# Gate and up projections as seven half-size products per unit in place of eight, and the down projection in four parts

## The chip, the cores and the metric

The kernel runs on one core of a Trainium2 chip. The metric is the device time of one execution in microseconds. The engines are named as in the profile: PE is the matrix engine (PEld its weight loads), DVE the vector engine, ACT the scalar engine, POOL the general-purpose engine, SP the engine that issues most transfers.

## The reference

One inference step of a decoder trunk with two layers, 1024 channels and 576 tokens (512 of a prompt, 64 of samples), all in float32:

```python
for l in range(2):
    x = x + 0.5 * swiglu(rms_norm(x, ffn1_norm[l]), ffn1_w_gu[l], ffn1_w_down[l])
    # l = 0: dilated attention and causal pooling between one input and one output projection
    # l = 1: gated width-3 convolution between two projections
    x = x + mixer(rms_norm(x, mix_norm[l]))
    x = x + 0.5 * swiglu(rms_norm(x, ffn2_norm[l]), ffn2_w_gu[l], ffn2_w_down[l])
y = rms_norm(x, final_norm)

def swiglu(x, w_gu, w_down):             # w_gu 1024 x 5632, w_down 2816 x 1024
    g, u = jnp.split(x @ w_gu, 2, axis=-1)
    return (jax.nn.silu(g) * u) @ w_down
```

So there are four SwiGLU halves, called F1 to F4 here, in the order F1, mixer (attention and pooling), F2, F3, convolution, F4, final norm.

## The kernel before

Activations lie feature-major: `x` is [128 channels, 8 channel tiles, 576 tokens]. Every product runs in reduced-precision float32 passes on exact splits: a weight tile w is split into wh (a cast on ACT, L61) and wl = w − wh (a subtraction on DVE, L62), the activations likewise into `xh` (ACT, L161) and `xl` (DVE, L162), and each product is the three passes wh·xh + wh·xl + wl·xh. A matmul has a 128 x 128 weight and 288 tokens (`C`), so a full product of 1024 input channels and 128 output channels is 8 channel tiles x 3 passes x 2 token halves = 48 matmuls (`proj` and `part`, L220).

A SwiGLU half (`ffn`) has 22 hidden tiles j of 128 channels. For each j there is one 48-matmul product for gate and one for up. `evac` multiplies both by the token factor r of the RMS norm, applies SiLU and multiplies them (L264 to L267), and splits the result into `hh` (ACT) and `hl` (POOL, L269). After 11 hidden tiles come 8 output tiles d of the down projection, 66 matmuls each (11 hidden tiles x 3 x 2), whose result is added to x with the factor one half (L294). So a SwiGLU half is 2 x (11 x 96 + 8 x 66) = 3168 matmuls. In the second half of it, each d also gives its squares to POOL and its split for the next phase to ACT and DVE (`split_x`).

The norm's factor is not needed for the product itself, since it multiplies the result. `norm` sums the squares over channels with four matmuls on PE (L183) and takes the root on ACT and DVE. It is called behind the first product of a phase, and its result is first used in `evac`. In F1 the program start does this by token tiles instead (`tok_factor`, `first_factors`), and the first two products run channel tile by channel tile while x comes in (`first_pair`, L239).

The order of the work on each engine is the order in which the code is written; each engine takes its instructions in that order and waits where a tile is not ready. Weights come by `Weights.load` on SP into two buffers of 1 MB, and are split two tiles ahead of their use. PSUM holds four accumulators of two banks. The last two output tiles of F4 are done by token halves (`last_down`, L330), so that the final norm of the first half lies beside the products of the second.

Of the kernel before, what the change touches and what calls it, by code (L numbers as in the profile page):

```python
# [26 lines left out]
NEG = -1e36  # L27
TOKS = [slice(128 * j, min(128 * j + 128, NT)) for j in range(5)]
# [4 lines left out]
class Weights:  # L33
    """The stream of weight tiles in order of use: loads run ahead, splits two chunks ahead."""

    def __init__(self, nc, raw_pool, split_pool, units):
        self.nc, self.raw_pool, self.split_pool = nc, raw_pool, split_pool
        self.units = units
        self.chunks = []
        for u, (ap, cols, parts) in enumerate(units):  # L40
            o = 0
            for n in parts:
                self.chunks.append((u, o, n, o + n == cols))
                o += n
        self.raw = {}
        self.ready = {}
        self.last = None
        self.n_load = self.n_split = self.n_used = 0
# [7 lines left out]

    def tiles(self):
        return [self.split_pool.tile([128, 1024], F32R, tag=n, name=n) for n in ("wh", "wl")]

    def parts(self, src, h, l, v):  # L60
        self.nc.scalar.copy(out=h[:, v], in_=src)  # L61
        self.nc.vector.tensor_tensor(out=l[:, v], in0=src, in1=h[:, v].bitcast(F32), op=ALU.subtract)  # L62

    def first(self):
        """the first unit, a quarter of both its chunks at a time: (load, split)"""
        ap = self.units[0][0].rearrange("p (c n) -> p c n", c=2)
        t = self.raw_pool.tile([128, 2048], F32, tag="raw", name="raw").rearrange("p (c n) -> p c n", c=2)
        self.ready = {c: self.tiles() for c in range(2)}
        self.n_load, self.n_split = 1, 2

        def load(i):
            v = slice(256 * i, 256 * i + 256)
            self.nc.sync.dma_start(out=t[:, :, v], in_=ap[:, :, v])

        def split(i):
            v = slice(256 * i, 256 * i + 256)
            for c in range(2):
                self.parts(t[:, c, v], *self.ready[c], v)

        return load, split  # L80

    def split(self):
        u, o, n, last = self.chunks[self.n_split]
        if u not in self.raw:
            self.load()
        final = self.last is not None and self.n_split == len(self.chunks) - 1
        h, l = self.ready[self.n_split] = self.last if final else self.tiles()
        self.parts(self.raw[u][:, o:o + n], h, l, slice(0, n))
        self.n_split += 1
        if last:  # L90
            del self.raw[u]
            self.load()

    def next(self, ahead=2):
        while self.n_split <= min(self.n_used + ahead, len(self.chunks) - 1):
            self.split()
# [3 lines left out]


def ch(t):
    """[p, 576] as [p, 2, 288]"""
# [3 lines left out]
class Trunk:  # L107
    def __init__(self, ctx, tc, I, O, phases):
# [5 lines left out]
        self.ps = ctx.enter_context(tc.tile_pool(name="ps", bufs=4, space=PSUM))  # L114
# [6 lines left out]
        self.gain = cp.tile([128, 7, KD], F32, name="gain")  # L121
        self.ones = cp.tile([128, 128], F32, name="ones")
# [5 lines left out]
        g = lambda ap: ap.rearrange("p a b -> p (a b)")  # L128
# [1015 lines left out]
```

## Time and profile before

| | before |
|---|---|
| median of three runs | 2355.4 us |
| the three runs | 2355.1, 2355.4, 2358.45 us |
| profiled execution, span of its instructions | 2358.6 us |
| profiled execution, outside the span | the page shows nothing there; the slowest of the runs is about as long as the span |
| PE busy | 98% of the span |
| DVE, ACT, POOL busy | 45%, 27%, 21% |
| mean granted clock of PE | 0.993 |
| moved by transfers | 217.89 MB |

Busy shares are averages over the whole span. PE works nearly without a break, so what sets the time is the number of matmuls and how closely they follow each other, and every pause of PE adds to the end. The mean duration of one matmul in the profile (some 0.3 us) overlaps its neighbours; the step from one start to the next is what a matmul costs.

### The profile page before, as it was taken

The page shows a single profiled execution, that of the slowest core. Times are in us where ns is not written, and L with a number is a line of the kernel's source. Part 1 is how long each engine was busy: PE and PEld are TensorE (multiplying, and loading weights), DVE is VectorE, ACT ScalarE, POOL GpSimd, SP SyncE. Part 2 cuts the span into 40 slices and gives each one's busy share as a digit, 9 for nine tenths or more (in the row PEclk, how much of TensorE's full clock was granted, in tenths as well). Part 3 has the DMA queues.
Part 4 walks back from the last instruction along what each step waited for, and adds up shares of the span by engine and source line. Part 5 has one row for each costly group of instructions (what it writes and reads, how often), then busy time and mean ns, then how long its engine had stood idle before and what let it go on. Part 6 is the DMA issues. An engine that isn't in the chain of part 4 may idle for free.

```text
span 2358.6 us, 39984 instructions
## 1 busy us (share of the span) xinstructions
PE 2323.2 (98%) x17517; PEld 2292.0 (97%) x17517; DVE 1067.6 (45%) x1462; ACT 635.3 (27%) x965; POOL 498.1 (21%) x490
## 2 busy tenths in 40 slices
PE   8999999999999999999999999999999999999998
PEld 8999999999888899999999999999999999999998
DVE  5432344526666754333435533333554563323334
ACT  4221222223334332212222322222221232212222
POOL 2100012308555641100113010011322231000112
PEclk9999999999999999999999999999999999999999
DMA  4222212443334422223222222221222222222222
GB/s 149 75 75 93 90 67 76 154 157 106 127 126 138 130 72 90 79 74 108 72 69 103 85 71 74 102 78 67 98 91 72 91 79 83 73 82 93 85 69 70
DMA packets 70910, 217.89 MB, mean 92 GB/s; under 512 B 14224, under 2 KB 37776, under 8 KB 54096
## 3 DMA queue, kind: packets, MB, share of 16 engines
q1 hardware_dynamic: 70304, 215.24, 27.5%
q8 instruction: 137, 2.24, 0.4%
q14 instruction: 37, 0.30, 0.0%
q10 hardware_dynamic: 432, 0.10, 0.0%
HBM read 204.22 MB, written 11.10 MB: 91 GB/s over the span
## 4 chain that ended last, share of the span: by engine, by line
PE 93%; DVE 5%; issue 1%; POOL 1%; DMA 0%; ACT 0%; SPq 0%; POOLq 0%; DVEq 0%; ACTq 0%
PE acc L220 86%; PE acc L651 3%; PE acc L749 1%; DVE wl L62 1%; DVE U L776 1%; DVE P L804 1%; PE acc L763 1%; PE acc L655 0%; PE acc L849 0%; PE acc L239 0%; DVE xl L162 0%; PE acc L330 0%; PE acc L826 0%; DVE me L789 0%; DMA raw<-in_gu 0%
## 5 line engine op out<-in xcount | busy, mean ns | idle before, releaser
L220 PE MATMUL acc<-xh,wh 128*128 128x288 f32 x3744 | 804.4, 296 | 0.0
L220 PE MATMUL acc<-xl,wh 128*128 128x288 f32 x3744 | 801.9, 295 | 0.4 <-POOL xl L996 0.4
L220 PE MATMUL acc<-xh,wl 128*128 128x288 f32 x3744 | 801.9, 295 | 0.0
L62 DVE TENSOR_TENSOR wl<-raw,wh 128x1024 fp32r<-128x1024 f32 (+3 forms) x389 | 517.0, 1331 | 573.1 <-ACT wh L61 572.0
L220 PEld LDWEIGHTS acc<-xh,wh 128*128 128x128 f32 x3744 | 603.8, 188 | 4.3 <-ACT P L741 1.8
L220 PEld LDWEIGHTS acc<-xl,wh 128*128 128x128 f32 x3744 | 604.1, 188 | 0.7 <-POOL xl L996 0.6
L220 PEld LDWEIGHTS acc<-xh,wl 128*128 128x128 f32 x3744 | 604.2, 188 | 0.0
L61 ACT CAST wh<-raw 128x1024 fp32r<-128x1024 f32 (+3 forms) x389 | 367.0, 945 | 680.8 <-PE acc L220 613.4
L269 POOL TENSOR_TENSOR hl<-t,hh 128x576 fp32r<-128x576 f32 x88 | 126.1, 1433 | 1287.6 <-ACT hh L268 1258.5
L220 PE MATMUL acc<-hl,wh 128*128 128x288 f32 x1364 | 292.1, 296 | 0.0
L220 PE MATMUL acc<-hh,wl 128*128 128x288 f32 x1364 | 292.1, 296 | 0.0
L220 PE MATMUL acc<-hh,wh 128*128 128x288 f32 x1364 | 292.0, 296 | 0.0
L220 PEld LDWEIGHTS acc<-hh,wl 128*128 128x128 f32 x1364 | 219.8, 189 | 0.0
L220 PEld LDWEIGHTS acc<-hh,wh 128*128 128x128 f32 x1364 | 219.8, 189 | 0.0
L220 PEld LDWEIGHTS acc<-hl,wh 128*128 128x128 f32 x1364 | 219.7, 189 | 0.0
L266 DVE TENSOR_TENSOR t<-acc,r 128x576 f32<-128x576 f32 x88 | 66.7, 758 | 312.6 <-PE acc L220 312.6
L268 ACT CAST hh<-t 128x576 fp32r<-128x576 f32 x88 | 59.3, 674 | 397.0 <-DVE t L267 397.0
L294 DVE SCALAR_TENSOR_TENSOR x<-acc,x 128x576 f32<-128x576 f32 x62 | 47.0, 758 | 159.1 <-PE acc L220 159.1
L265 ACT ACTIVATE t<-t 128x576 f32<-128x576 f32 x88 | 60.3, 686 | 179.2 <-DVE t L264 179.2
L156 POOL TENSOR_TENSOR sqt<-x 128x576 f32<-128x576 f32 x33 | 37.9, 1149 | 184.1 <-DVE x L294 158.8
L161 ACT ACTIVATE xh<-x,gain 128x576 fp32r<-128x576 f32 x48 | 36.9, 776 | 141.5 <-DVE x L294 101.4
L267 DVE TENSOR_TENSOR t<-t,t 128x576 f32<-128x576 f32 x88 | 66.8, 759 | 9.2
(220 smaller groups left out, 1581.4 us busy)
## 6 DMA issues: line engine op xcount, KB each, us to landing
raw<-in_gu SPq DMA_DIRECT2D x87, 1024.0 KB, 4.9
raw<-in_dn SPq DMA_DIRECT2D x64, 704.0 KB, 4.1
raw<-in_wqk SPq DMA_DIRECT2D x12, 1024.0 KB, 4.9
raw<-in_cv SPq DMA_DIRECT2D x12, 1024.0 KB, 4.9
kv<-in_kb SPq DMA_DIRECT2D x32, 256.0 KB, 4.3
kv<-in_vb SPq DMA_DIRECT2D x32, 256.0 KB, 4.7
raw<-in_wv SPq DMA_DIRECT2D x6, 1024.0 KB, 5.2
raw<-in_wo SPq DMA_DIRECT2D x4, 1024.0 KB, 4.8
```

What stands on the lines that cost most here:

```text
L61: self.nc.scalar.copy(out=h[:, v], in_=src)
L62: self.nc.vector.tensor_tensor(out=l[:, v], in0=src, in1=h[:, v].bitcast(F32), op=ALU.subtract)
L156: nc.gpsimd.tensor_tensor(out=t, in0=self.x[:, k, :], in1=self.x[:, k, :], op=ALU.mult)
L161: nc.scalar.activation(out=self.xh[:, k, :], in_=self.x[:, k, :], func=AF.Copy, scale=gcol)
L220: nc.tensor.matmul(out=p[:, c, :C], lhsT=w, rhs=m[:, k0 + k, c * C:c * C + C], start=(first and k == 0 and z == 0), stop=(last and k == kn ...
L265: nc.scalar.activation(out=t1, in_=t1, func=AF.Silu)
L266: nc.vector.tensor_tensor(out=t2, in0=pu[:, :, :C], in1=r, op=ALU.mult)
L267: nc.vector.tensor_tensor(out=t2, in0=t2, in1=t1, op=ALU.mult)
L268: nc.scalar.copy(out=ch(hh[:, j, :]), in_=t2)
L269: nc.gpsimd.tensor_tensor(out=ch(hl[:, j, :]), in0=t2, in1=ch(hh[:, j, :].bitcast(F32)), op=ALU.subtract)
L294: nc.vector.scalar_tensor_tensor(out=xd, in0=p[:, :, :C], scalar=0.5, in1=xd, op0=ALU.mult, op1=ALU.add)
L651: nc.tensor.matmul(out=outs[i], lhsT=self.tok(x[:, kk, :], toks[i]), rhs=w, start=(kk == 0 and z == 0), stop=(kk == 7 and z == 2))
```

## The change

The 1024 x 256 block of weights of a hidden tile (gate and up side by side) and the 1024 x 576 activations are each cut into 2 x 2 blocks: 512 input channels by 128 output channels, and 512 input channels by 288 tokens. The product of two such blocked matrices is formed with seven block products in place of eight. The activation side needs seven "forms", sums and differences of the blocks of x (B11, B21, B22 and T1 to T4), each split into a high and a low part. They are made once for a SwiGLU half. The weight side needs sums of the four weight blocks (`sums`), made for every hidden tile on DVE, and their splits: a (two plain blocks), e and f (two sums each), and d (`dsplit`, one plain block).

A hidden tile is now a `unit` of seven block products of 12 matmuls each (`seven`, L352): 84 matmuls in place of 96. In a steady unit their order is B11, T4 of the unit before, B21, T1, T2, B22, T3. Bank 0 of the accumulator x takes B11 and then B21 on top (`a`), bank 1 takes T1 and then B22 (`f`), and a separate bank B takes a copy of B11's result made by ACT (L392), and then T2, T3 and T4 on top. So gate of the first token half is `a`, and the three others are sums of what the banks hold at different times; ACT copies `f` and B aside in between (L416, L418). `gate0` (L399) reads `a` on DVE. In the first unit of each part there is no unit before, and the order is B11, T1, B21, T2, B22, T3, with `gate0` behind T2 in the code.

The down projection is done in four parts (CHUNKS, of 5, 5, 6 and 6 units), each with 8 output tiles d of 30 or 36 matmuls. The first two d leave out the last unit's hidden tile until T4 of it is done. The result of a d is multiplied by `rm` (a row of −r/2, since h carries the other sign) and added to x by two DVE instructions (L504, L505) in place of one. The norm's factor comes by token tiles in every SwiGLU half (`factor_sums`, `newton`, `factor`), inside its first unit. Squares are on ACT, their sums on POOL. PSUM is three accumulators of two banks and two single banks.

```diff
+CHUNKS = ((0, 5), (5, 5), (10, 6), (16, 6))
...
+    def sums(self, u):
...
+        tt(out=b[:, 0:2], in0=r[:, 0:4:2], in1=r[:, 2:4], op=ALU.add)
+        tt(out=b[:, 2], in0=b[:, 1], in1=r[:, 0], op=ALU.add)
+        tt(out=b[:, 3], in0=b[:, 2], in1=r[:, 1], op=ALU.add)
...
+    def dsplit(self, u):
+        h, l = (self.dpool.tile([128, 512], F32R, tag=n, name=n) for n in ("dh", "dl"))
+        self.parts(self.raw[u][:, 1536:2048], h, l)
...
+    def hi_lo(self, hl, src, g):
...
+        nc.scalar.activation(out=hl[0], in_=src, func=AF.Copy, scale=g)
+        nc.vector.scalar_tensor_tensor(out=hl[1], in0=src, scalar=g, in1=hl[0].bitcast(F32), op0=ALU.mult, op1=ALU.subtract)
+    def forms_low(self, k, n, xb, tmp, eng=None):
...
+        self.hi_lo(self.form("B11", k), x0, g)
+        nc.scalar.activation(out=xb, in_=x1, func=AF.Copy, scale=g)
+        (eng or nc.vector).tensor_tensor(out=tmp, in0=x0, in1=x1, op=ALU.subtract)
+        self.hi_lo(self.form("T1", k), tmp, g)
+    def forms_high(self, k, n, xb, st):
...
+        self.hi_lo(self.form("B21", k), x0, g)
+        stt(out=st[:, 0], in0=x1, scalar=g, in1=xb, op0=ALU.mult, op1=ALU.subtract)
+        stt(out=st[:, 1], in0=self.x[:, k, :C], scalar=ngk, in1=st[:, 0], op0=ALU.mult, op1=ALU.subtract)
+        stt(out=st[:, 2], in0=x0, scalar=ng, in1=st[:, 1], op0=ALU.mult, op1=ALU.subtract)
+    def forms_main(self, k, n, st):
...
+        nc.scalar.copy(out=h, in_=st)
+        nc.vector.tensor_tensor(out=l, in0=st, in1=h.bitcast(F32), op=ALU.subtract)
+        self.hi_lo(self.form("B22", k), self.x[:, k + 4, C:], self.gain[:, n, k + 4:k + 5])
...
+    def seven(self, out, name, w, col, first, last):
...
+        for k in range(4):
+            v = slice(col + 128 * k, col + 128 * k + 128)
+            fh, fl = self.form(name, k)
+            for z, (a, m) in enumerate(((h, fh), (h, fl), (l, fh))):
+                nc.tensor.matmul(out=out, lhsT=a[:, v], rhs=m, start=(first and k == 0 and z == 0),
+                                 stop=(last and k == 3 and z == 2), skip_group_check=True)
+    def half_mult(self, s):
...
+        tt(out=s["h"][:, C:], in0=s["B"][:, :C], in1=s["p5"], op=ALU.add)
+        tt(out=s["h"][:, C:], in0=s["h"][:, C:], in1=s["g"][:, C:], op=ALU.mult)
+    def finish_unit(self, s):
...
+        self.seven(s["B"][:, :C], "T4", s["d"], 0, False, True)
+        nc.vector.tensor_tensor(out=s["h"][:, :C], in0=s["B"][:, :C], in1=s["g"][:, :C], op=ALU.mult)
+    def unit(self, u, j, prev, fresh, start):
...
+        x = self.acc()
+        a, f, b = x[:, 0, :C], x[:, 1, :C], self.psb.tile([128, 512], F32, tag="B", name="B")
...
+        if prev:
+            self.half_mult(prev)
+        wa = W.take()
+        self.seven(a, "B11", wa, 0, True, False)
+        W.ahead(1)
+        nc.scalar.copy(out=b[:, :C], in_=a)
+        if prev:
+            self.finish_unit(prev)
+            s["d"] = W.dsplit(u)
+            self.hidden_parts(prev)
+        def gate0():
+            tt(out=g0, in0=a, in1=r[:, :C], op=ALU.mult)
+            nc.scalar.activation(out=g0, in_=g0, func=AF.Silu)
+        if prev:
+            self.seven(a, "B21", wa, 512, False, True)
+            gate0()
+        we = W.take()
+        self.seven(f, "T1", we, 0, True, False)
+        if start:
+            self.factor_sums()
+        if not prev:
+            s["d"] = W.dsplit(u)
+            self.seven(a, "B21", wa, 512, False, True)
+        W.sums(u + 1)
+        W.ahead(1)
+        if start:
+            self.newton(*self.fa)
+        nc.scalar.copy(out=s["p5"], in_=f)
+        self.seven(b[:, :C], "T2", we, 512, False, False)
+        nc.scalar.copy(out=u2, in_=b[:, :C])
+        if start:
+            self.factor()
+        if not prev:
+            gate0()
+        wf = W.take()
+        self.seven(f, "B22", wf, 512, False, True)
+        tt(out=g1, in0=f, in1=u2, op=ALU.add)
+        tt(out=g1, in0=g1, in1=r[:, C:], op=ALU.mult)
+        W.ahead(1)
+        nc.scalar.activation(out=g1, in_=g1, func=AF.Silu)
+        self.seven(b[:, :C], "T3", wf, 0, False, False)
...
+    def factor(self):
...
+        self.spread(outs, f, TOKS)
+        nc.scalar.copy(out=self.r[:, 0:512], in_=p[:, 0, :])
+        nc.scalar.copy(out=self.r[:, 512:], in_=p[:, 1, :64])
+        nc.vector.tensor_scalar(out=self.rm, in0=self.r, scalar1=-0.5, scalar2=None, op0=ALU.mult)
...
+    def ffn(self, i, u0):
...
+            self.half_mult(s)
+            held = []
...
+            for d in range(8):
...
+                if d < 2:
+                    self.down_part(p, w, 0, kc - 1, kc)
+                    held.append((d, p, w))
+                    if d == 0:
+                        self.finish_unit(s)
+                        self.hidden_parts(s)
+                        s = None
+                        continue
+                    for d, p, w in held:
+                        self.down_part(p, w, kc - 1, 1, kc)
+                else:
+                    self.down_part(p, w, 0, kc, kc)
+                    held = [(d, p, w)]
+                for d, p, w in held:
+                    self.down_out(d, p, last, nxt, kind)
...
+    def down_out(self, d, p, last, nxt, kind):
...
+        nc.vector.tensor_tensor(out=ch(t), in0=p[:, :, :C], in1=ch(self.rm), op=ALU.mult)
+        nc.vector.tensor_tensor(out=xd, in0=xd, in1=t, op=ALU.add)
```

How the instructions stand on an engine is decided by this code's order. Three places on DVE follow. First, a steady unit (the second and third of F1). Before, for each hidden tile, with two weight tiles' subtractions (L62), the two evacuations and their product:

```order
L62 TENSOR_TENSOR wl<-raw,wh 128x1024 x2
L264 TENSOR_TENSOR t_544<-acc,r 128x576
L266 TENSOR_TENSOR t_545<-acc,r 128x576
L267 TENSOR_TENSOR t_545<-t_545,t_544 128x576
L62 TENSOR_TENSOR wl<-raw,wh 128x1024 x2
```

After, from the subtraction of f of one unit (sum, `wl`) over the evacuation of T4 (L365), the subtraction of d, `gate0` (L399), the sums for the next unit (L103 to L105), the subtraction of the next a, the evacuation of B22 (L425, L426), the subtraction of the next e, and the addition that opens the next unit (L358):

```order
L93 TENSOR_TENSOR wl<-sum,wh 128x1024
L365 TENSOR_TENSOR h<-B,g 128x288
L93 TENSOR_TENSOR dl<-raw,dh 128x512
L399 TENSOR_TENSOR g<-acc,r 128x288
L103 TENSOR_TENSOR sum<-raw 128x1024
L104 TENSOR_TENSOR sum<-sum,raw 128x512
L105 TENSOR_TENSOR sum<-sum,raw 128x512
L93 TENSOR_TENSOR wl<-raw,wh 128x1024
L425 TENSOR_TENSOR g<-acc,u_384 128x288
L426 TENSOR_TENSOR g<-g,r 128x288
L93 TENSOR_TENSOR wl<-sum,wh 128x1024
L358 TENSOR_TENSOR h<-B,p_383 128x288
```

Five instructions per hidden tile have become thirteen (L359, a product behind L358, is not among these rows), and `gate0`, for which PE's T1 waits (it writes the other bank of the same accumulator), stands behind T4's evacuation and d's subtraction.

Second, the end of F2, where x is prepared for F3. Before, for one output tile d: its evacuation (L294), its split (L162), and the subtractions of the weights that come next:

```order
L62 TENSOR_TENSOR wl<-raw,wh 128x768
L62 TENSOR_TENSOR wl<-raw,wh 128x640
L294 SCALAR_TENSOR_TENSOR x<-acc,x 128x576
L162 SCALAR_TENSOR_TENSOR xl<-x,gain,xh 128x576
L62 TENSOR_TENSOR wl<-raw,wh 128x1024 x2
L294 SCALAR_TENSOR_TENSOR x<-acc,x 128x576
```

After, for an output tile of the upper four (d = 4 to 7), with evacuation (L504, L505), three combinations (L245 to L247) that need ACT's copy `xb` of the lower tile, the low parts of the forms (L227, L253) and the weights' subtraction:

```order
L504 TENSOR_TENSOR dt<-acc,rm 128x576
L505 TENSOR_TENSOR x<-x,dt 128x576
L227 SCALAR_TENSOR_TENSOR exl<-x,gain,exh 128x288
L245 SCALAR_TENSOR_TENSOR st<-x,gain,xb 128x288
L246 SCALAR_TENSOR_TENSOR st<-x,ngain,st 128x288
L247 SCALAR_TENSOR_TENSOR st<-x,ngain,st 128x288
L253 TENSOR_TENSOR xl<-st,xh 128x864
L227 SCALAR_TENSOR_TENSOR xl<-x,gain,xh 128x288
L93 TENSOR_TENSOR wl<-raw,wh 128x768
```

Two instructions for x have become eight, and L253 stands behind a cast on ACT that itself waits for L247.

Third, the norm's factor in the first unit of F3. Before, with L179 to L172 behind the last weights' subtraction, and `evac` (L264) at the end:

```order
L62 TENSOR_TENSOR wl<-raw,wh 128x1024
L179 TENSOR_TENSOR sql<-sq,sqh 128x576
L185 TENSOR_SCALAR ms<-acc 128x576
L169 RECIPROCAL r<-r 128x576
L170 TENSOR_TENSOR nt<-r 128x576
L171 SCALAR_TENSOR_TENSOR nt<-nt,ms 128x576
L172 SCALAR_TENSOR_TENSOR r<-nt,r 128x576
L62 TENSOR_TENSOR wl<-raw,wh 128x1024
L264 TENSOR_TENSOR t_12444<-acc,r 128x576
```

After, behind the addition of epsilon (L308) and d's subtraction: the sums of the next unit, its a, the root's refinement (L279 to L282), the rows that PE turns (L319), `rm` (L455) and `gate0` (L399):

```order
L103 TENSOR_TENSOR sum<-raw 128x1024
L104 TENSOR_TENSOR sum<-sum,raw 128x512
L105 TENSOR_TENSOR sum<-sum,raw 128x512
L93 TENSOR_TENSOR wl<-raw,wh 128x1024
L279 RECIPROCAL fr<-fr 128x5
L280 TENSOR_TENSOR fr<-fr 128x5
L281 SCALAR_TENSOR_TENSOR fr<-fr 128x5
L282 SCALAR_TENSOR_TENSOR fr<-fr 128x5
L319 TENSOR_SCALAR ft<-ones,fr 128x128 x4
L319 TENSOR_SCALAR ft<-ones,fr 64x128
L455 TENSOR_SCALAR rm<-r 128x576
L399 TENSOR_TENSOR g<-acc,r 128x288
```

Before, nothing but one weight tile lay between the factor and its use. Now the next unit's sums and its subtraction lie ahead of the refinement, and PE's product B22 of the first unit is written behind all of it, since it waits for `gate0`.

## Rows read from the trace of the kernel before

**Rows 1.** The page: the span, and section 1 (busy time, share, instructions).
```profile
span 2358.6 us, 39984 instructions
...
PE 2323.2 (98%) x17517; PEld 2292.0 (97%) x17517; DVE 1067.6 (45%) x1462; ACT 635.3 (27%) x965; POOL 498.1 (21%) x490
```
**Rows 2.** The chain that ended last, in order of time: start us, us, what.
```profile
35.42 404.98 PE acc L220 x3036
...
876.57 422.37 PE acc L220 x3168
1298.93 0.53 PE acc L183 x4
...
1927.67 398.37 PE acc L220 x2988
```
**Rows 3.** Timeline, all engines, around the last product: start, us, engine, line, what, [idle before].
```profile
2319.34 1.42 POOL L157 TENSOR_TENSOR sq<-sq,sqt 128x576 f32<-128x576 f32 x1
...
2319.61 1.97 DVE L62 TENSOR_TENSOR wl<-raw,wh 128x768 fp32r<-128x768 f32 x1 [1.58 <-ACT wh L61]
...
2325.87 0.29 PE L330 MATMUL acc<-hh,wh 128*128 128x288 f32 x1
...
2326.00 0.30 PE L330 MATMUL acc<-hl,wh 128*128 128x288 f32 x1
...
2326.07 0.76 DVE L294 SCALAR_TENSOR_TENSOR x<-acc,x 128x576 f32<-128x576 f32 x1 [2.63 <-PE acc L220]
```
**Rows 4.** The chain again, where PE waits for a weight's split near the end.
```profile
2330.02 0.97 DVE wl L62
...
2331.03 5.95 PE acc L330 x43
```
**Rows 5.** Groups by line and form, DVE: busy us, mean ns | idle before, releaser.
```profile
L62 DVE TENSOR_TENSOR wl<-raw,wh 128x1024 fp32r<-128x1024 f32 x254 | 366.9, 1446 | 399.6 <-ACT wh L61 398.5
L62 DVE TENSOR_TENSOR wl<-raw,wh 128x768 fp32r<-128x768 f32 x64 | 92.9, 1451 | 35.1 <-ACT wh L61 35.1
L267 DVE TENSOR_TENSOR t<-t,t 128x576 f32<-128x576 f32 x88 | 66.8, 759 | 9.2
...
L162 DVE SCALAR_TENSOR_TENSOR xl<-x,gain,xh 128x576 fp32r<-128x576 f32 x48 | 48.9, 1035 | 28.4 <-ACT xh L161 28.4
...
L411 DVE TENSOR_TENSOR t<-t,y 128x512 f32<-128x512 f32 x8 | 5.5, 692 | 0.3
...
L957 DVE TENSOR_TENSOR rot<-acc,r 128x288 f32<-128x288 f32 x4 | 1.8, 450 | 0.0
```
**Rows 6.** Groups by line and form, ACT, same columns.
```profile
L61 ACT CAST wh<-raw 128x1024 fp32r<-128x1024 f32 x254 | 265.2, 1045 | 413.3 <-PE acc L220 351.5 <-PE acc L655 35.3 <-issue 25.7
...
L829 ACT COPY PT<-acc 128x512 f32<-128x512 f32 x16 | 9.4, 585 | 38.8 <-PE acc L826 38.8
...
L340 ACT ACTIVATE xg<-x,gain 128x288 f32<-128x288 f32 x4 | 2.1, 537 | 9.1 <-DVE x L336 9.1
```
**Rows 7.** Timeline of the first 36 us: POOL, then DVE, then PE.
```profile
9.62 4.67 POOL L449 TENSOR_TENSOR sq<-x 128x576 f32<-128x576 f32 x3 [0.37 <-DMA x<-in_x]
14.25 3.14 POOL L454 TENSOR_TENSOR sq<-sq,sq 128x576 f32<-128x576 f32 x2
...
13.20 2.92 DVE L62 TENSOR_TENSOR wl<-raw,wh 128x256 fp32r<-128x256 f32 x2
...
18.65 0.75 DVE L62 TENSOR_TENSOR wl<-raw,wh 128x256 fp32r<-128x256 f32 x2
...
31.21 2.36 DVE L62 TENSOR_TENSOR wl<-raw,wh 128x1024 fp32r<-128x1024 f32 x2 [0.15 <-ACT wh L61]
33.48 1.06 DVE L206 TENSOR_SCALAR ft<-ones,fr 128x128 f32<-128x128 f32 x5
...
18.06 0.85 PE L239 MATMUL acc<-xl,wh 128*128 128x288 f32 x2 [2.86 <-DVE xl L162]
```
**Rows 8.** Windows: length, busy time by engine (x instructions), granted clock, DMA share, GB/s.
```profile
18.00:20.00 2.00, 1.94 (x8) 1.95 (x9) 2.00 (x5) 1.85 (x2) 0.00 (x0) 0.50 0.00 0
```

More of the change, by code (lines that the diff above doesn't have):

```diff
@@ L55, in load, with need @@
             self.nc.sync.dma_start(out=t[:, :cols], in_=ap)
+    def need(self, u):
+        while u >= self.n_load:
+            self.load()
+        return self.raw[u]
     def tiles(self):
         return [self.split_pool.tile([128, 1024], F32R, tag=n, name=n) for n in ("wh", "wl")]
-    def parts(self, src, h, l, v):
-        self.nc.scalar.copy(out=h[:, v], in_=src)
-        self.nc.vector.tensor_tensor(out=l[:, v], in0=src, in1=h[:, v].bitcast(F32), op=ALU.subtract)
     def first(self):
[L66 to L80, printed above, removed]
@@ L82, in split @@
-    def split(self):
[L83 to L88, printed above, removed]
-        self.n_split += 1
[L90 to L95, printed above, removed]
+        t = self.raw[0] = self.raw_pool.tile([128, 2048], F32, tag="raw", name="raw")
@@ new lines, in split @@
+    def split(self):
+        if self.n_split >= len(self.groups):
+            return
+        u, k = self.groups[self.n_split]
+        if k in ("e", "f") and self.spool is None:
+            return
+        h, l = self.ready[self.n_split] = self.tiles()
+        self.n_split += 1
+        blocks = lambda t: t.rearrange("p (b n) -> p b n", b=2)
+        if k == "a":
+            self.parts(self.need(u)[:, 0:1024], h, l)
+        elif k == "e":
+            self.sums(u)
+            self.parts(self.sum[u][:, 512:1536], h, l)
+        elif k == "f":
+            src = self.sum.pop(u).rearrange("p (b n) -> p b n", b=4)[:, 0:4:3]
+            self.parts(src, blocks(h), blocks(l))
+        else:
+            o, n, last = k
+            self.parts(self.need(u)[:, o:o + n], h[:, :n], l[:, :n])
+            if last:
+                self.release(u)
@@ L99, in next @@
         return r
+    def next(self, ahead=2):
+        self.ahead(ahead)
+        return self.take()
 def ch(t):
@@ new lines, in down_part @@
+    def down_part(self, p, w, k0, kn, kc):
+        nc = self.nc
+        h, l = w
+        for k in range(k0, k0 + kn):
+            wh, wl = (t[:, 128 * k:128 * k + 128] for t in (h, l))
+            for z, (a, m) in enumerate(((wh, self.hh), (wh, self.hl), (wl, self.hh))):
+                for c in range(2):
+                    nc.tensor.matmul(out=p[:, c, :C], lhsT=a, rhs=m[:, k, c * C:c * C + C],
+                                     start=(k == 0 and z == 0), stop=(k == kc - 1 and z == 2))
@@ new lines, in down_out @@
+    def down_out(self, d, p, last, nxt, kind):
+        nc, tp = self.nc, self.tp
+        t = tp.tile([128, NT], F32, tag="dt", name="dt")
+        xd = self.x[:, d, :]
+        nc.vector.tensor_tensor(out=ch(t), in0=p[:, :, :C], in1=ch(self.rm), op=ALU.mult)
+        nc.vector.tensor_tensor(out=xd, in0=xd, in1=t, op=ALU.add)
+        if not last:
+            return
+        self.square(d, tp)
+        if kind == "ffn":
+            self.forms(d, nxt, tp)
+        elif kind == "final":
+            nc.scalar.activation(out=self.xg(d), in_=xd, func=AF.Copy, scale=self.gain[:, 6, d:d + 1])
+        else:
+            self.split_x(d, nxt)
@@ L416, in conv @@
             nc.scalar.dma_start(out=self.O["conv_s"], in_=os)
+            self.open_forms()
+            self.xb = [tp.tile([128, C], F32, tag="xb", name="xb", bufs=4) for _ in range(4)]
             for d in range(KD):
```

372 lines of the change are left out of this document (229 added, 143 removed).

## The prediction

> **What bounds the kernel now.** I read the page first: PE is busy 98% of a span of 2358.6 us and DVE 45% [rows 1]. The chain of work that ended last then shows what a matmul costs: a whole SwiGLU half is one unbroken piece of 3168 matmuls in 422.37 us, so 0.1333 us each, and the norm's four matmuls between two halves stand there with 0.53 us [rows 2]. The reader is to see that nothing but PE's count sets the time inside a half and that even the change of halves costs half a microsecond. So any matmul taken away is worth 0.133 us, and any pause put in costs its full length. The runs of 2355.1 to 2358.45 us lie at or up to 3 us below the span, so a sum made against 2358.6 may come out 0.1% above a median.
>
> **The change part by part.**
>
> *Products.* 88 hidden tiles lose 12 of 96 matmuls: 1056 x 0.1333 = −140.8 us. Two things differ from the main run of L220: each matmul has a weight of its own, and twelve in a row go to one bank. The last products before (L330) are of that kind already: their starts stand 0.13 us apart [rows 3]. I charge nothing. The nearest row against it is 43 such matmuls in 5.95 us behind a pause, 0.138 each [rows 4]; were that the step, the 7392 new ones would cost 37 us more.
>
> *A steady unit (72 of 88).* PE works 84 x 0.1333 = 11.2 us. T1 writes bank 1 of the accumulator whose bank 0 `gate0` reads, and the tile is tracked as one, so T1 waits until `gate0` is done, and that can start only when B21 is complete. The price: 0.20 us from the next matmul's possible start to DVE's first read behind a product (2325.87 to 2326.07, [rows 3]), 0.45 for a 288-column evacuation (L957, [rows 5]), 0.04 from DVE's end to PE's start (2330.99 to 2331.03) and 0.1 for the refill (the 43 matmuls took 0.2 more than 43 x 0.1333) [rows 4]. That is 0.8 us per unit, 72 x 0.8 = +57.6. The bounds are 0.5 (half the handover hidden by the pipeline) and 1.0. The copies that ACT makes (L392, L416, L418: between 0.4, scaled from 512 columns in 0.585, and 0.54 [rows 6]) have a product of 1.6 us in between and cost nothing. They would cost some 0.7 each without it.
>
> DVE has 13 instructions in a unit: three subtractions of 1024 and a first sum of 1024 at 1.18 (two in 2.36, [rows 7]), three of 512 at 0.69, and six of 288 at 0.45 [rows 5]. That is 9.5 us clean, and 10.5 at the mean of 1.446 that the subtractions have beside POOL. A unit lasts 12.0 us, so DVE stays below. The tightest place is the addition L358 for T4: behind the evacuation of B22 (ready at 10.6 of 12.0), two instructions of 0.45 and a subtraction of 1.2 it ends at 13.15, and T4 wants it at 13.6. That cover is 0.45 us.
>
> *The first unit of parts 2 to 4 (12 units).* There is no T4 to lie between. T1 waits for ACT's copy of B11's result (0.2 + 0.4 + handover = 0.75), and B22 waits for `gate0`, which in DVE's order stands behind what the last output tile and the unit leave there: e (to 1.85 us from B11's start), the evacuation of d = 7 (two at 0.76, to 3.4), f, d, three sums, the next a, `gate0` (9.6). PE has reached 0.75 + 4 x 1.6 = 7.15. So 0.75 + 2.4 = 3.2; I take 3.0, with 2.1 and 5.0 as ends (the upper one with a clock drop, below): +36.
>
> *The four starts.* Three things are new. (i) T1 waits for ACT's copy of B11, which stands behind the casts of all forms and of f; so T1 comes after DVE's whole work on the forms and two weight sums. (ii) From T1 to B22 runs the norm's chain, and `gate0` is its last link: T1 1.6, the root and other small steps 2.0 (five small instructions took 1.06, [rows 7]), d 0.7, the sums 2.6, a 1.2 to 1.45, the rows to be turned 1.06, the turning 0.6, copies 0.8, `rm` 0.55, `gate0` 0.45, some ten handovers 1.5: 13.5 us, in which PE has T1, B21 and T2, 4.8 us. Loss 8.7 (6.7 to 9.7). (iii) After a pause of 2.86 us PE ran at half clock: 0.50 granted, the 1.2 GHz level, and 8 matmuls in 2 us where 15 would go [rows 7, 8]. I charge 2 us per start.
>
> When T1 comes, by a list of DVE's instructions in their order, at 0.5 us for a 288-column form (half of 1.035), 1.1 for 864 columns, 0.76 for 576 [rows 5], 0.9 where DVE waits for ACT's cast of 864 columns (L61 by columns, [rows 6]):
> - Program start. DVE has 23 us, from about 6 us on. POOL has six squares at 1.56, seven sums at 1.57 [rows 7] and four subtractions, some 23 us, and beside POOL two subtractions of 256 took 2.92 us where alone they take 0.75 [rows 7]. With DVE at half speed until 28 us, T1 is at 41 (34 to 48). PE has then done 1.6 us of work, so it is 39.4 behind; before, it had done 132 matmuls (17.6 us) at 35.42 [rows 2], 17.8 behind. +21.6 + 8.7 + 2 = +32.
> - F2, from the mixer's last product: the last tile's forms, the four `forms_main`, sums and e: T1 at 14. 14 − 1.6 + 8.7 + 2 − 0.5 (what the change of halves cost before) = +22.6.
> - F3: each d now gives PE 36 x 0.1333 = 4.8 us, but DVE 4.0 to 4.8 for the lower four (evacuation 1.52, three forms 1.5, a weight subtraction of 0.95 to 1.45 [rows 5]) and 7.1 for the upper four (1.52, 2.5, the wait for ACT 0.9, 1.1, a weight subtraction). Starting at 9.6, when d = 0 and 1 come together, DVE ends at about 57, and with sums and e at 61 to 66; PE ends at 38.4. T1 at 28 (20 to 33): +36.6.
> - F4: 48 matmuls (6.4 us) per d cover more. DVE is some 4 us late at the end; T1 at 15: +23.6.
>
> Sum of the starts +115 (75 to 150).
>
> On POOL beside DVE, the Trainium skill's page "SBUF — State Buffer" (section "SBUF: two separate sides") says that a DVE instruction with two inputs in SBUF and a GpSimd instruction take a shared port pair as an exclusive lock, and the loser fully blocks. The rows agree in kind: 1.97 us for a subtraction of 768 columns beside a POOL sum, 0.97 without [rows 3, 4]. By the full rule the program start would have DVE's 23 and POOL's 23 us one behind the other, T1 at 52 and a total 11 us higher; I stay with the mix of the rows, since DVE's waits for ACT leave POOL time that costs nothing.
>
> *Smaller.* In the last part of F1 and F3 the additional instruction, the square on ACT and the weight's subtraction make 5 us of DVE per d against 4.8 of PE, and the first two d come together: +13 for both mixers' entries. Tail (one instruction more per half, shorter cover) and the eight small matmuls that open bank B: +3.
>
> Sum: −140.8 + 57.6 + 36 + 115 + 13 + 3 = +83.8, 2442 us.
>
> **The rivals.**
> - *Faster: the starts are hidden.* Place: DVE's queue between the last down product and B22 of a SwiGLU half's first unit. For it: PE's last part of a down projection is 38 us long, and ACT and POOL are free. Against it: DVE's order as listed, and the norm's chain, which no product of PE covers. The other terms add 110 us, so the kernel is faster by more than 0.2% only if the four starts together cost under 26 us, 6.5 each, less than the norm's chain alone. At no cost it would be 2327.
> - *Half hidden:* steady pauses of 0.5 (−22) and starts of 75 (−40): 2380; with the twelve first units at 2.1 (−11) and nothing for the mixers' entries (−13), 2356: slower, at its end the same.
> - *Slower still:* DVE's margin of 0.45 us in a steady unit goes where its instructions meet POOL's 1.43 us subtraction, T4 then waits some 0.3 (+22), and the twelve first units drop the clock (+24): 2490.
> - *The products don't cost what is said:* 0.138 in place of 0.133, 2479. [rows 3] speak against it.
>
> **How the numbers follow.** Changes under 0.2% (4.7 us) are about what a measurement of this kernel can't tell from none. My forecast (2400 to 2475) gets 0.56, half hidden 0.18 (of it 0.03 within 0.2%), faster 0.10, slower still 0.11, dearer products 0.05. So faster 0.10, same 0.03, slower 0.87. The range of 2370 to 2500 leaves out the faster cases and the ends of the bounds. The likeliest case alone has 2400 to 2475.
>
> **What would show it.** In the profile after, PE's new groups should sum to 1056 matmuls less; the waits of PE should name L399 with about 0.75 us some 72 times (T1) and some 16 times with 2 us or more (B22), and ACT's L392 in 16 first units. Windows over a steady stretch should show 7 products per 12.0 us. The four starts should each show PE idle for 20 us or more in two pieces, at a clock of 0.5 behind them. A SwiGLU half's inner part, without its start, should be shorter than before, by some 12 us. I am wrong if T1 doesn't wait, if the inner part gains 30 us, or if DVE is ready with the forms when PE ends the last down product.

## The result and the profile after

The change made the kernel slower: 2469.95 us (median of 4 runs, 2468.32 to 2474.56) against 2356.85 us (median of 4), a ratio of 1.048 (95% interval 1.0465 to 1.0495). The forecast was 2442 us with a range of 2370 to 2500. The profiled execution has a span of 2472.8 us against 2358.6, 114.2 us more.

The page of the changed kernel, span and section 1, answers to [rows 1]:

```profile
span 2472.8 us, 39729 instructions
...
PE 2257.6 (91%) x16508; PEld 2195.5 (89%) x16508; DVE 1634.6 (66%) x2477; ACT 940.8 (38%) x1593; POOL 448.6 (18%) x461
```

PE has some 1000 instructions less and is busy 91% in place of 98%: the span lost matmuls and gained pauses. What PE waits for (engine and line, what it waited for: us in total, times, longest):

```profile
PE acc L352 <- ACT B L392: 75.6, 16, 31.4
PE acc L352 <- DVE g L399: 68.8, 88, 2.1
PE acc L439 <- ACT wh L92: 10.4, 4, 4.9
...
PE acc L322 <- DVE ft L319: 8.1, 4, 3.1
...
PE acc L333 <- DVE dt L504: 3.9, 1, 3.9
```

Both kinds of wait that the prediction named are there: `gate0` (L399) 88 times, once in every unit, and the copy of B11 (L392) in the 16 first units. The prediction had 2 us or more for `gate0` in 16 of them; it was 2.1 us in eight, 1.7 to 1.8 in the four starts and 1.3 in the other four. Next the chain over one steady unit (start us, us, what):

```profile
83.26 1.86 PE acc L352 x12
85.12 1.58 PE B L352 x12
86.70 1.58 PE acc L352 x12
88.28 1.60 PE B L352 x12
89.88 1.60 PE acc L352 x12
91.48 1.60 PE B L352 x12
93.08 1.61 PE acc L352 x12
94.69 0.02 issue
94.72 0.47 DVE g L399
95.19 0.04 issue
95.23 0.79 PE acc L352 x4
```

Twelve matmuls take 1.58 to 1.61 us (1.86 right behind the wait), so the step of 0.133 us of [rows 2] holds for the new products. From T1 (83.26) to the next T1 (95.23) it is 11.97 us, of which 11.2 is work and 0.77 is what the wait for `gate0` costs, the slow first matmuls behind it included (PE itself stands idle for 0.55).

The start of F3, from the same view: the evacuations (dt, L504) of the lower tiles d = 1 to 3 and of d = 4, the forms of a tile of the upper four (d = 5) from one dt to the next, and T1 and B22 of the first unit:

```profile
1318.97 0.68 DVE dt L504
...
1326.46 0.68 DVE dt L504
...
1333.18 0.68 DVE dt L504
...
1339.96 0.68 DVE dt L504
...
1348.96 0.68 DVE dt L504
1349.64 0.02 issue
1349.67 0.77 DVE x L505
1350.47 0.04 issue
1350.52 0.68 ACT sqt L263
1351.20 0.43 ACT exh L226
1351.64 0.03 issue
1351.66 1.41 DVE exl L227
...
1358.20 0.68 DVE dt L504
...
1378.84 3.25 PE acc L352 x12
...
1393.24 2.96 PE acc L352 x12
```

The reader is to see that a tile of the lower four takes 6.7 to 7.5 us (1318.97 to 1326.46 to 1333.18 to 1339.96) and one of the upper four 9.0 to 9.2 (to 1348.96, to 1358.20), that DVE stands still for the square (L263) and the cast behind it (L226) on ACT, that a low part of 288 columns takes 1.41 us, and that T1 and B22 (the last two rows) take 3.25 and 2.96 us for twelve matmuls in place of 1.60, at a granted clock of 0.50 (1379 to 1382) and 0.54 (1393.3 to 1396).

The same sum as in the prediction. Each loss is the distance between two products less the matmuls between them at 0.1333 us, and less what the kernel before lost at the same place:

| term | forecast | measured | from |
|---|---|---|---|
| products | −140.8 | −140.8 | twelve in 1.60 |
| steady units | 57.6 | 55.4 | 72 x 0.77 |
| 12 first units of later parts | 36 | 45.4 | 8 x 4.57 and 4 x 2.2 |
| four starts | 115 | 131.4 | 38.4, 22.3, 44.4, 26.3 |
| mixers' entries | 13 | 20.3 | 10.6 and 9.7 |
| tail and rest | 3 | 2.5 | what is left |
| sum | 84 | 114.2 | span +114.2 |

For F3's start, for example: from T1 of F2's last unit (1297.19) to B22 (1393.24) are 96.05 us and 396 matmuls (52.8), so 43.2 lost, and another 1.7 behind B22 at half clock; the norm of the kernel before cost 0.5 here (2.6 at F2's start). For F4's: from the end of the convolution's last product (2016.0) to B11 of the second unit (2052.4) are 36.4 us and 72 matmuls (9.6), less 0.5. The entries are the losses from T1 of the last unit of F1 and F3 to the end of its down projection (4.6 and 4.1) and what the two mixers took longer than before (6.0 and 5.6).

### The profile page after: what moved, and what is told of

The parts are those of the page before. It is cut to its first block, busy times and chain, and to the rows that moved or that the text cites. A ratio compares the mean times of both kernels' runs of the same rounds, so it can differ in the third digit from the quotient of the medians.

```text
span 2472.8 us, 39729 instructions
## 1 busy us (share of the span) xinstructions
PE 2257.6 (91%) x16508; PEld 2195.5 (89%) x16508; DVE 1634.6 (66%) x2477; ACT 940.8 (38%) x1593; POOL 448.6 (18%) x461
## 4 chain that ended last, share of the span: by engine, by line
PE 79%; DVE 14%; ACT 3%; issue 2%; POOL 1%; DMA 1%; SPq 0%; POOLq 0%; ACTq 0%; DVEq 0%
PE acc L352 23%; PE acc L439 18%; PE B L352 17%; PE acc L333 14%; PE acc L918 3%; DVE wl L93 3%; DVE g L399 2%; DVE exl L227 1%; DVE x L505 1%; DVE dt L504 1%; DVE sum L103 1%; ACT wh L92 1%; PE acc L1016 1%; DVE U L1043 1%; ACT sqt L263 1%
## 5 line engine op out<-in xcount | busy, mean ns | idle before, releaser
L352 PE MATMUL acc<-exh,wh 128*128 128x288 f32 x1056 | 327.0, 310 | 119.1 <-ACT B L392 75.6
L352 PEld LDWEIGHTS acc<-exh,wh 128*128 128x128 f32 x1056 | 202.4, 192 | 141.1 <-ACT B L392 79.6
L352 PE MATMUL acc<-exl,wh 128*128 128x288 f32 x1056 | 317.1, 300 | 1.8 <-DVE exl L227 1.8
L352 PE MATMUL acc<-exh,wl 128*128 128x288 f32 x1056 | 315.7, 299 | 0.7 <-DVE wl L93 0.7
L93 DVE TENSOR_TENSOR wl<-sum,wh 128x1024 fp32r<-128x1024 f32 x176 | 216.4, 1230 | 7.4 <-ACT wh L92 7.4
L352 PE MATMUL B<-xh,wh 128*128 128x288 f32 x704 | 212.1, 301 | 0.0
L333 PE MATMUL acc<-xh,wh 128*128 128x288 f32 x960 | 208.4, 299 | 3.9 <-DVE dt L504 3.9
L352 PE MATMUL B<-xl,wh 128*128 128x288 f32 x704 | 211.5, 300 | 0.0
L352 PE MATMUL B<-xh,wl 128*128 128x288 f32 x704 | 210.8, 299 | 0.0
L333 PE MATMUL acc<-xl,wh 128*128 128x288 f32 x960 | 206.5, 296 | 0.8 <-POOL xl L1263 0.7
L333 PE MATMUL acc<-xh,wl 128*128 128x288 f32 x960 | 206.1, 296 | 0.0
L352 PEld LDWEIGHTS acc<-exl,wh 128*128 128x128 f32 x1056 | 203.0, 192 | 2.8 <-DVE exl L227 2.8
```

Source lines behind the costliest of these rows:

```text
L93: self.nc.vector.tensor_tensor(out=l, in0=src, in1=h.bitcast(F32), op=ALU.subtract)
L333: nc.tensor.matmul(out=p[:, c, :C], lhsT=w, rhs=m[:, k0 + k, c * C:c * C + C], start=(first and k == 0 and z == 0), stop=(last and k == kn ...
L352: nc.tensor.matmul(out=out, lhsT=a[:, v], rhs=m, start=(first and k == 0 and z == 0), stop=(last and k == 3 and z == 2), skip_group_check= ...
```

## The experiments

Ratios are to the kernel before, timed on the same chip beside each run; 0.001 is 2.4 us. The changed kernel has 1.048. What a run is said to gain or lose in us is the difference of two ratios, since the runs were on several chips; the difference of two medians can be 2 or 3 us off it.

**1. `gate0` early in first units.** One part of DVE's order is changed.

```diff
             self.seven(a, "B21", wa, 512, False, True)
+            if not start:
+                gate0()
         W.sums(u + 1)
...
-        if not prev:
+        if start:
             gate0()
```

> In the first unit of parts 2 to 4 the evacuation of the first gate (L399 of the changed kernel) is written right behind B21 instead of behind the next unit's sums and its next weight subtraction. Theory (DVE's order holds B22 back): the 12 waits of 2.1 us go, and with them the drop to half clock behind 8 of them (some 1.6 us each): 12 x 2.1 + 8 x 1.6 = 38 us less than the changed kernel, about 2432 us. Rival (DVE is late anyway, from the last output tile and the subtractions of f and d): under 10 us less, above 2460 us.

2447.26 us, 1.0373 (1.0355 to 1.039): 25 us less, between the two. Its waits of PE:

```profile
PE acc L352 <- DVE g L399: 46.7, 76, 1.8
...
PE acc L352 <- ACT p L418: 8.2, 12, 0.7
```

The 12 waits for L399 are gone, 22 us. In their place B22 waits 0.7 us for ACT's copy of T1's result, which stands behind the next weight's cast, and in the four first units behind a part of six the pause had been only 1.3 us with no clock drop. So the order on DVE was the cause, and the size was overrated.

**2. T1 and B22 in another accumulator.**

```diff
         x = self.acc()
-        a, f, b = x[:, 0, :C], x[:, 1, :C], self.psb.tile(
+        y = self.xprev if prev else x if start else self.acc()
+        self.xprev = x
+        a, f, b = x[:, 0, :C], y[:, 1, :C], self.psb.tile(
```

> T1 and B22 go to the second bank of the accumulator of the unit before (in the first unit of parts 2 to 4 to an accumulator of its own), so that no tile is read by the evacuation of the first gate while PE wants to write its other bank; first units of a SwiGLU half are unchanged. Theory (the wait is one of tiles, not of data): T1's 0.77 us goes in 76 units (58 us), and in the 12 first units of later parts both pauses and the clock drops go (45 us): about 2370 us, a steady unit 11.2 us. Rival (DVE, with 9.5 us of work and only 0.45 us of cover ahead of T4, takes over): the wait comes back at T4 or T1 as a wait for DVE, a steady unit 11.6 us or more, above 2400 us.

2379.77 us, 1.0089 (1.0074 to 1.0104): 92 us less. The chain of this kernel, T1 of one unit and of the next:

```profile
925.26 1.60 PE acc L352 x12
926.86 1.60 PE B L352 x12
928.46 3.20 PE acc L352 x24
...
936.42 1.60 PE acc L352 x12
```

A unit takes 11.16 us, without a pause; DVE does the same 13 instructions beside it. The wait was one of tiles: no data in the second bank had anything to do with `gate0`. The rival, DVE as the bound, falls: it keeps up in 11.16 us too. Only the 12 first units have a new wait, 0.6 us for L358 (7.0 us in all), which is most of what is missing to the theory's 2370.

**3. The norm's chain ahead of the sums.** The edit reached further than its expectation says: the order of the sums and the next a was turned in every unit, not only in the first one.

```diff
-        W.sums(u + 1)
-        W.ahead(1)
         if start:
             self.newton(*self.fa)
+            self.factor_rows()
+        W.ahead(1)
+        W.sums(u + 1)
...
```

> In the first unit of each SwiGLU half the refinement of the root and the rows to be turned (DVE) stand ahead of the next unit's sums and its next weight subtraction, which are then done while PE and ACT turn and copy the factors. Theory (DVE's order makes the chain long): 2.6 + 1.2 us of work and two pauses of 0.57 us leave the chain, part of it comes back behind it: 3.5 to 5 us less per half, 14 to 20 us in all, about 2453 us. Rival (the chain is set by the clock of PE and by ACT, or the late sums hold the next unit back): under 6 us less, above 2464 us.

2503.36 us, 1.0612 (1.0596 to 1.0627): 31 us more, and neither theory. The chain in F1's start, (start us, us, what):

```profile
51.70 2.05 issue
53.75 1.06 ACT wh L92
54.81 0.02 issue
54.84 1.23 DVE wl L93
56.06 1.14 DVE sum L103
```

The next a's cast (ACT) starts only at 53.75, and with the sums behind it in its order DVE has nothing to do until then; before, the sums filled that time. The waits for L399 grew by 30 us (68.8 to 98.3), in the first units of the later parts above all, and B22 of F1 starts at 59.53 as it did (59.66). So this run doesn't tell what the chain alone is worth; it shows that in the later parts' first units the sums are better placed ahead of the next a.

**4. Forms ahead of squares on ACT.**

```diff
-        self.square(d, tp)
         if kind == "ffn":
             self.forms(d, nxt, tp)
...
             self.split_x(d, nxt)
+        self.square(d, tp)
...
+                self.forms(d, nxt, tp)
                 self.square(d, tp)
-                self.forms(d, nxt, tp)
```

> Behind the last part of a down projection and behind the convolution's output projection the square of an output tile (ACT) is written behind the forms or the split of x instead of ahead of them. Theory (at the ends of the phases DVE waits in each output tile for ACT's 0.68 us square and the cast behind it): some 0.7 us x 8 tiles at F2's end, up to that much at the two mixers' entries, less at the convolution's end where DVE has some 1.6 us more per tile: 10 to 18 us less, about 2456 us. Rival (DVE's own work or POOL's sums, which then meet other DVE instructions, set the end): within 4 us of the changed kernel, 2466 us or more.

2470.31 us, 1.0472 (1.0457 to 1.0488): no difference that the medians tell, as the rival said. The profile suggests why: F4's last `gate0` starts 6.8 us earlier (2401.51, and 2408.27 in the changed kernel), and the span is only 3.3 us shorter (2469.5), since the same move had been made in F4, where the squares are on the path of the final norm. The profiled execution of the changed kernel was 4.6 us longer than its median, so this alone would not show it; run 6, which leaves F4 out, bears it out with a gain of 6 to 7 us.

**5 to 9. Towards a faster version, one wait at a time,** each on top of the one before, beginning with run 2. First the start: own accumulators, the chain ahead of the sums, and the rows turned behind T3 (`factor_turn` is the second half of `factor`):

```diff
...
+            self.seven(f, "B22", wf, 512, False, True)
+            self.seven(b[:, :C], "T3", wf, 0, False, False)
+            self.newton(*fa)
+            self.factor_rows()
+            self.a_ahead(u + 1)
+            self.half_add(s)
+            W.sums(u + 1)
+            self.factor_turn()
+            gate0()
+            W.ahead(1)
...
```

> On top of the own accumulator for T1 and B22 (2379.8 us, 1.009 of before): in the first unit of each SwiGLU half too the two banks are in two tiles, and the rows to be turned are turned behind T3 instead of behind T2, so that T2, B22 and T3 lie beside the norm's chain; in DVE's order the chain stands ahead of the next unit's sums. Theory (B22 waits for the chain only through the tile and the order): of the 8 to 9 us that each start loses between T1 and B22 6 to 8 go: 24 to 32 us less, 2348 to 2356 us. Rival (the chain itself, from POOL's sum of squares over root, turning and copies, then holds T4 or T1 of the next unit by as much): under 10 us less, above 2370 us.

2378.43 us, 1.0085 (1.007 to 1.01): as run 2, so the rival, though the wait came back at B21 and not at T4 or T1. PE's waits show where the chain went:

```profile
PE acc L352 <- ACT B L395: 45.0, 6, 19.6
PE acc L352 <- ACT wh L92: 33.6, 5, 10.9
```

At the starts B22 no longer waits for `gate0`, and B21 of the second unit waits instead, for ACT's copy of B11. The timeline of F1's start, PE and then ACT (start us, us, what; in brackets the idle time ahead and what ended it):

```profile
64.54 0.61 PE L352 MATMUL acc<-exh,wh 128*128 128x288 f32 x1 [4.95 <-ACT B L395]
```

```profile
59.28 0.44 ACT L403 ACTIVATE g<-g 128x288 f32<-128x288 f32 x1 [1.37 <-DVE g L402]
59.63 1.03 ACT L92 CAST wh<-sum 128x1024 fp32r<-128x1024 f32 x1
62.81 0.44 ACT L432 ACTIVATE g<-g 128x288 f32<-128x288 f32 x1 [2.15 <-DVE g L431]
63.16 1.03 ACT L92 CAST wh<-sum 128x1024 fp32r<-128x1024 f32 x1
64.10 0.39 ACT L395 COPY B<-acc 128x288 f32<-128x288 f32 x1
```

The copy (last row) is queued on ACT behind both SiLUs of the first unit, which wait for DVE's norm, and behind the casts of e and f. Then the order of run 4, without F4:

```diff
+        if kind == "final":
+            self.square(d, tp)
...
+        if kind != "final":
+            self.square(d, tp)
...
```

> The kernel of the run with the start reordered, and the square of an output tile behind its forms or split on ACT in F1 to F3 and the convolution, but not in F4. Theory (the same reordering alone had saved 6.8 us up to F4's first unit and lost 3.5 us of them behind F4's last tiles, where the sum of squares is on the path): 6 to 7 us less than with the start reordered alone. Rival (POOL's sums and DVE's own work set the ends): within 2 us of it.

2372.29 us, 1.0054 (1.0039 to 1.0069): 7 us less by the ratios and 6 by the medians, as the theory said. Then the second step of the forms behind the next tile's first:

```diff
-            self.forms_main(d - 4, nxt, st)
+            if d > 4 and eng is None:
+                self.forms_main(d - 5, nxt, self.st)
+            self.st = st
+            if d == 7 or eng is not None:
+                self.forms_main(d - 4, nxt, st)
```

> As the run before this one, and the forms' second step (the cast of 864 columns on ACT, the low part of 864 and B22's form on DVE) of an output tile written behind the first step of the next tile, at the ends of F1's mixer excepted. Theory (DVE waits 0.92 us for that cast in each of the upper four tiles): three such waits less at F2's end and at the convolution's end, at most 6 us less. Rival (DVE's own work then stands there): within 2 us.

2366.05 us, 1.0032 (1.0022 to 1.0042): 5 us less by the ratios and 6 by the medians, as the theory said. Then e and the copy of T1's result earlier:

```diff
             W.sums(u + 1)
+            self.ahead_of(u + 1, "e")
             self.factor_turn()
             gate0()
-            W.ahead(1)
...
+        nc.scalar.copy(out=s["p5"], in_=f)
         if not prev:
             gate0()
         W.sums(u + 1)
         W.ahead(1)
-        nc.scalar.copy(out=s["p5"], in_=f)
```

> On top of the forms' second step behind the next tile's first (2366.1 us, 1.0032 of before): the next unit's e is cast and split ahead of the factors' copies (in the three runs before this, PE waited 5.2 us for it in the second unit of each SwiGLU half, which ate what the reordered start had given), and ACT copies T1's result aside ahead of the next weight cast, for which B22 waited 0.8 us in 12 first units. Theory: 4 x 4 to 5 us and 12 x 0.8 us less, 2338 to 2342 us, 0.993 of before, so faster than the kernel before. Rival (the waits move on, to the evacuations that DVE then does later, or to gate of the first unit): less than 10 us, above 2356 us, no faster than before.

2360.59 us, 1.0006 (0.9997 to 1.0015): 6 us less, nearer to the rival. The expectation had named e's cast as what holds the second unit up, and that was only a part: with e's cast moved away, B21 at F1 still waits 3.88 us (4.95 in run 5) for the copy of B11, behind the two SiLUs and f's cast. A part of that is a table that ACT loads straight ahead of the first SiLU, 1.28 us (59.47 to 60.75). So the copy goes ahead of all that:

```diff
+        late = prev and "silu" in prev
...
+        if prev and not late:
+            W.ahead(1)
         nc.scalar.copy(out=b[:, :C], in_=a)
+        if late:
+            for g in prev["silu"]:
+                nc.scalar.activation(out=g, in_=g, func=AF.Silu)
...
```

> On top of the run with e ahead of the copies (2360.6 us, 1.0006 of before): in the first two units of each SwiGLU half ACT copies B11's result into bank B ahead of the cast of f, and in the second unit ahead of the first unit's two SiLUs too. Theory (in the second unit B21 waited 4.2 us for that copy, which on ACT stood behind the SiLUs, and these behind the norm's chain; in the first unit B21 waited behind the cast of f): 3 to 4 us less in each second unit and 0.5 to 1 us in each first: 14 to 20 us less, 2341 to 2347 us, 0.993 to 0.996 of before. Rival (the chain reaches PE at another place, at T4 or T1 of the second unit): under 5 us less, 2356 us or more.

2345.68 us, 0.9943 (0.993 to 0.9955): 15 us less, as the theory said, and faster than before.

**10. Sums of squares on DVE.** The changed kernel with one thing moved.

```diff
-            nc.gpsimd.tensor_tensor(out=self.sq, in0=self.sq, in1=t, op=ALU.add)
+            if not dve:
+                nc.gpsimd.tensor_tensor(out=self.sq, in0=self.sq, in1=t, op=ALU.add)
+                return
+            if k > 1:
+                nc.vector.tensor_tensor(out=self.sq, in0=self.sq, in1=self.t_sq, op=ALU.add)
+            self.t_sq = t
...
-        self.square(d, tp)
+        self.square(d, tp, kind != "final")
...
```

> The changed kernel, but the sums of squares behind the last parts of F1 to F3 and behind the convolution are made by DVE, one tile late, instead of by POOL (28 additions of 576 columns). Theory (a POOL addition holds up the DVE instruction with two inputs in SBUF beside it for as long as it runs: 1.4 us in place of 0.5 for a form's low part): DVE gets 0.76 us more of its own per tile and loses 0.7 to 1.0 of waiting: within 6 us of the changed kernel, 2464 to 2476 us, with the low parts of the forms at 0.5 us each. Rival (DVE's long instructions only fill time in which it would have waited for ACT): the 28 additions come on top, 28 x 0.76 = 21 us, above 2485 us.

2451.59 us, 1.0389 (1.0373 to 1.0405): 21 us less, better than either. The low parts of a form and of a split, first in the changed kernel, then in this one (DVE groups by form):

```profile
L227 DVE SCALAR_TENSOR_TENSOR exl<-x,gain,exh 128x288 fp32r<-128x288 f32 x32 | 34.1, 1065 | 24.4 <-ACT exh L226 24.3
L269 DVE SCALAR_TENSOR_TENSOR xl<-x,gain,xh 128x576 fp32r<-128x576 f32 x16 | 22.2, 1390 | 23.3 <-ACT xh L268 23.3
```

```profile
L227 DVE SCALAR_TENSOR_TENSOR exl<-x,gain,exh 128x288 fp32r<-128x288 f32 x32 | 21.3, 666 | 15.6 <-ACT exh L226 15.6
...
L276 DVE SCALAR_TENSOR_TENSOR xl<-x,gain,xh 128x576 fp32r<-128x576 f32 x16 | 13.1, 818 | 13.7 <-ACT xh L275 13.7
```

These two groups lose 22 us of duration, as much as the 28 additions cost DVE (28 x 0.76), and 18 us of waiting for ACT, since the additions stand where DVE had waited. Both readings of the expectation were half right, and together they are the gain.

**11 and 12.** Run 9 with the same sums on DVE, and then the mixer's squares and sums moved likewise (`gpsimd` to `scalar` and `vector` in its `sq`).

```diff
...
-            self.square(d, tp)
+            self.square(d, tp, True)
...
```

> The run with the copies first (2345.7 us, 0.9943 of before) and the sums of squares behind F1 to F3 and the convolution on DVE, one tile late, instead of on POOL. Theory (POOL's additions hold DVE up at these four ends; moving them alone had given 20 us): 10 to 18 us less here, where squares no longer stand ahead of the forms and part of the same waiting is gone already: 2328 to 2336 us, 0.987 to 0.991 of before. Rival (the two measures fill the same waits): under 5 us less.

2334.11 us, 0.9896 (0.9879 to 0.9912): 11 us less than run 9, in the theory's range, and 1.0% faster than the kernel before.

```diff
-            nc.gpsimd.tensor_tensor(out=s, in0=t.x[:, k, :], in1=t.x[:, k, :], op=ALU.mult)
-            nc.gpsimd.tensor_tensor(out=t.sq, in0=t.sq, in1=s, op=ALU.add)
+            nc.scalar.activation(out=s, in_=t.x[:, k, :], func=AF.Square)
+            if k > 1:
+                nc.vector.tensor_tensor(out=t.sq, in0=t.sq, in1=t.t_sq, op=ALU.add)
...
```

> As the run before this one, and behind the mixer's output projection too the squares are made by ACT and the sums by DVE, one tile late, instead of both by POOL. Theory (there too low parts and combinations take 1.4 to 1.7 us beside POOL in place of 0.5, but each tile has 6.4 us of PE's work as cover, so only the last tile counts): 1 to 3 us less. Rival (DVE's eight additions come on top at the end, where nothing covers the last two): the same or up to 2 us more.

2335.69 us, 0.9906 (0.9889 to 0.9922): no difference that the intervals tell. What PE still waits for in run 11:

```profile
PE acc L359 <- ACT wh L92: 32.2, 4, 10.9
PE acc L359 <- ACT B L404: 23.5, 6, 18.7
```

These are the starts, T1 and B21 behind DVE's forms; the 18.7 is the program start.

## Why the prediction was right, and where its sizes were off

- *Products.* As forecast. The rival of dearer products falls (1.60 us for twelve).
- *Steady units.* Forecast 0.8 us by four rows, measured 0.77, at the place and by the cause named; run 2 shows that the cause is the tile that two banks share, since the wait goes when the banks are in two tiles and nothing takes its place. The extra wait of T4 that "slower still" had did not come. Of DVE's two figures there, 10.5 us takes the first sum at the subtractions' mean too; with the three subtractions alone it is 10.3, which changes nothing.
- *First units of later parts.* The step "3.0, with 2.1 and 5.0 as ends" was mis-sized: 4.6 us where PE fell to half clock behind a pause of 2.1 us (8 times), 2.2 where the pause was 1.3 us (4 times). The clock drop had been left to the upper bound. With 25.2 us lost in its steady and first units against 35.2 saved, a half's inner part got 10 us shorter, forecast 12.
- *The four starts.* The term "+115" was mis-sized and measured 131; these 16 us are over half of the miss of 30. Half of them are F3, 44.4 in place of 36.6. Two steps were too low there: "4.0 to 4.8 for the lower four" (its own terms add up to 4.0 to 4.5) was 6.7 to 7.5 us per tile (d = 1 to 3), and "7.1 for the upper four" was 9.0 to 9.2 (d = 4 and 5). The list of DVE's instructions had left out ACT's square, which stands ahead of the form's cast (0.68 us in the rows above; run 6, which moves it at four ends, gained 6 to 7 us), and had priced a low part at 0.5 us where POOL's addition makes it 1.4 (1.41 in the rows above; run 10). The norm's chain was right in kind (T1 to B22 is 14.4 us at F3, forecast 13.5). At the program start T1 came at 45.8, forecast 41 in a bound of 34 to 48. F2 came out as forecast (22.3 and 22.6). PE was idle for 20 us or more at F1 and F3, but for 17 at F2 and F4, where the prediction had 20 too.
- *The mixers' entries.* "5 us of DVE per d" was 5.3 to 5.6 in F3's last part (dt at 1791.97, 1797.27, 1802.84 and 1808.37), and the term of 13 measured 20.
- *The range.* The forecast of 2442 is 28 us below the median. The misses do not cancel, as nearly all of them are on the low side, so the result owes nothing to luck; it lies in the range because the starts (75 to 150) and the first units (2.1 to 5.0) stayed inside the bounds given for them.
- *POOL beside DVE.* By the Trainium skill's page "SBUF — State Buffer" (section "SBUF: two separate sides") a blocked instruction waits out the other one. Of that rule this case shows the direction and a size, 1.07 us in place of 0.67 on the mean of 32 and 1.39 in place of 0.82 on the mean of 16 (run 10); its full form had T1 at 52 us, and the measured 45.8 lies between that and the 41 that the mix of rows gave.
- *The rival "faster"* had said that the starts together must cost under 26 us. With the two-tile change alone they still decide: run 2 is at 1.0089, and only runs 9, 11 and 12, which take the starts apart, end below 1.

What stays open: run 3 doesn't isolate the norm's chain, so that how a start's 22 to 44 us divide between forms, chain and clock is read from the trace and not shown by a run; and the program start's last 19 us of waiting were not tried.

## What to carry to other kernels

A saving on the bound engine is worth its count only if the engines that feed it keep their distance: here 1056 matmuls (141 us) were outweighed by 255 us of pauses and half-speed matmuls in a kernel whose averages (DVE 66%, ACT 38%) look idle. Two banks of one accumulator tile were one thing to wait for; where one was read while the other was to be written, two tiles took no more of PSUM here and gave 92 us (run 2). When a wait is removed from an in-order queue, read what is queued behind it next: in runs 1, 5 and 8 a part of the freed time came back at the next copy or cast on ACT, and at the starts it was gained only when the copy was moved too (run 9).

## What the runs showed of the hardware

Behind a pause of 2.1 us (154.5 to 156.6) PE fell to the 1.2 GHz level (granted clock 0.61 in a stretch of 4 us behind it, some 14 matmuls at 0.24 us), while behind a pause of 1.3 us at the same place of a later part it stayed at 1.00. So it was in all eight first units with the longer pause and all four with the shorter, and in run 1, which leaves 0.7 us of the pause, none of the twelve fell. The windows, with the columns of [rows 8]:

```profile
157.00:161.00 4.00, 4.00 (x22) 4.00 (x21) 2.05 (x3) 1.42 (x3) 0.00 (x0) 0.61 0.00 0
...
364.00:368.00 4.00, 2.69 (x21) 2.54 (x20) 1.95 (x4) 1.78 (x3) 0.00 (x0) 1.00 0.35 150
```
